# Way to the first experts: normed rows on VectorE, and two modulation groups moved there

## The chip, the cores and the metric

The kernel runs on one core of a Trainium2 chip. The metric is the time of one execution on the device in microseconds, the median over repeated executions. A core has TensorE (PE, matrix products), VectorE (DVE), ScalarE (ACT), GpSimd (POOL) and SyncE (SP, which here only issues transfers), each with an instruction stream of its own, kept in step by semaphores. Sixteen DMA engines move data between main memory and the on-chip memory. In the profile's rows PEclk is the clock granted to TensorE, as a share of 2.4 GHz; 0.50 is its lower level, 1.2 GHz.

## The reference, cut to what matters

A network of two blocks of layers on 256 tokens and 256 context tokens of width 1024, in float32. Each layer of the first block is modulated by a condition vector, mixes (linear recurrence and differential attention in layer 0, windowed attention in layer 1), and ends in a mixture of 16 experts of which every token takes two:

```python
mod = (jax.nn.silu(c) @ w_ada + b_ada)[:, None, :]
mod_c = (jax.nn.silu(c_ctx) @ w_ada + b_ada)[None, None, :]
sh1, sc1, g1, sh2, sc2, g2 = jnp.split(mod, 6, axis=-1)
...
x = x + g1 * y
h2 = rms_norm(x, norm_ffn_g[layer]) * (1.0 + sc2) + sh2
...
tokens = jnp.concatenate([h2.reshape(-1, d_), hc2.reshape(-1, d_)], axis=0)
f = routed_moe(tokens, router_w, router_b, moe_w_gate[layer], moe_w_up[layer], moe_w_down[layer])
...
# routed_moe
aff = jax.nn.sigmoid(jnp.dot(h2d, router_w).astype(F32))
sel = (aff + router_b.astype(F32)).reshape(n_tok, N_GROUPS, EXPERTS_PER_GROUP)
group_score = jnp.sum(lax.top_k(sel, TOP_K)[0], axis=-1)
grp = jnp.argmax(group_score, axis=-1)
...
hid = jax.nn.silu(xblk @ w_gate[e]) * (xblk @ w_up[e])
return hid @ w_down[e]
```

The weights `ada_w` of a layer are 1024 x 6144, so the modulation of both layers is 50 MB of weights for two condition vectors. The modulation of layer 1 is not needed before layer 1.

## The kernel before

The weights come from main memory in tiles of 128 x 2048 float32 (1 MB) that share a pool `W` of 14 slots; `wload` issues every one of them on SP's queue, in the order of the program, and an issue waits until the slot it takes has been released. Larger buffers take slots of the same pool: `XG` (two), the broadcast rows `rows2` (two), the gate rows `g1`. A scheduler orders the instructions of each engine ahead of time from the order of the program and the dependences; at run time each engine runs its list in order.

A modulation group, `ada_group(layer, i)`, covers two of the six parts of a layer's modulation: 8 tiles of `ada_w`, four matmuls to a tile (`pm`, line 364, in float32, which takes two passes, so 8 records in the trace), sums to `M` on VectorE (367), four transposes (375) and small copies to the tiles `AT`, `BT`, `ST`, `GT`. Its stationary operand is `scT`, the silu of the two condition vectors, made once at the start by `ada_setup` from two small loads to `cT`. `layer0` holds the groups in a list `extra` and hands out pieces by `more(n)`, n pairs of tiles at a time: in the linear recurrence, and in the attention `diff_attn` before each of its four blocks of 128 queries (`more(3)`). In the attention a head is two score matmuls (`sp`, 965), exponentials (ScalarE, 974), a scaled copy (978), the difference of the two softmaxes (VectorE, 979), transposes (982), and the product with the values (`ob`, 986). The first eight heads have 512 keys, the last eight 256.

Behind the output projection X gets the gated result: `tt` (VectorE, 770), and the addition to X (771), for two of the four row tiles of the second half on GpSimd. The router takes X's transposes and squares (`router_half`), `rstd` (573), and the logits `lg` (575 to 579), and ScalarE makes the sigmoid `aff` (582). `x_gain` forms X times a gain row in `XG` on GpSimd (561). In `ffn` ScalarE multiplies `XG` by `rstd` (1169) and GpSimd adds the shift row (1171); the rows go to main memory as `h2d` (1173), from where the later experts gather theirs. In `route` VectorE finds the two experts of every token: `sel` (1002), comparisons `cmp` (1012, 1013), a mask `mk` (1024), and TensorE counts places from it (`pp`, 1032 to 1036). The first expert's rows are gathered by matmuls with a one-hot matrix `hu` (`first_x`, 1262), and then the experts run: gate `G`, up `U` and down `Y`, each weight tile split by ScalarE (`wh`, 188) and VectorE (`wl`, 189) into two parts, three matmuls for each product (209 to 211). `preload` issues the first 7 tiles of expert 0 early, four of gate and three of up.

Of the kernel before, what the change touches and what calls it, by code (L numbers as in the profile page):

```python
# [11 lines left out]
F32 = mybir.dt.float32  # L12
# [5 lines left out]
OP = mybir.AluOpType  # L18
AX = mybir.AxisListType

P = 128
# [65 lines left out]
class Kern:  # L87
# [233 lines left out]
    def ada_setup(self):  # L321
        nc, wk, a = self.nc, self.wk, self.a
# [5 lines left out]
        nc.vector.memset(self.scT, 0.0)  # L328
        nc.scalar.activation(self.scT[:, :, 0:2], cT, AF.Silu)
        self.gmix = self.C.tile([P, 2, 8], F32, name="gmix")  # L330
# [20 lines left out]
    def ada_group(self, layer, i, bank=False):  # L351

        nc, wk, ps = self.nc, self.wk, self.ps
# [3 lines left out]
        for k in range(8):  # L357
            w = self.wload(W, k, 1, i * 2048, 2048)
            if not bank and k % 2 == 0:
                pm = ps.tile([P, 512], F32, name="pm", tag="tp", bufs=self.tpb)  # L360
            elif bank and k == 0:
                pm = ps.tile([P, 512], F32, name="pm", tag="mm", bufs=2)
# [15 lines left out]
        for r in range(2):  # L378
            v = mT[:, :, :, r].rearrange("p c j -> p j c")
            T = lambda nm: self.C.tile([P, 8], F32, name="%s%d%d" % (nm, layer, r))  # L380
            h = lambda t: t.rearrange("p (j c) -> p j c", j=2)
# [203 lines left out]
    def layer0(self):  # L585
        nc, tc, a = self.nc, self.tc, self.a
        with ExitStack() as st:
# [14 lines left out]
            extra = [self.ada_group(l, i, l == 1) for l, i in ((0, 1), (0, 2), (1, 0), (1, 1), (1, 2))]  # L602
# [146 lines left out]
            for c in range(2):  # L749
# [18 lines left out]
                for t in range(4):  # L768
                    tt = wk.tile([P, 512], F32, name="tt", tag="t2", bufs=self.t2b)
                    nc.vector.tensor_tensor(tt, o[t], g1[t // 2][:, cs], op=OP.mult)  # L770
                    (nc.gpsimd if c and t % 2 else nc.vector).tensor_tensor(self.X[t][:, cs], self.X[t][:, cs], tt, op=OP.add)
# [168 lines left out]
    def diff_attn(self, qT, kT, va, Y, more):  # L940
# [16 lines left out]
        for t in range(4):  # L957
            more(3)
# [31 lines left out]
    def route(self, NT, CB):  # L990
# [53 lines left out]
        nc.vector.tensor_copy(mxi,mx)  # L1044

# [99 lines left out]
    def ffn(self, layer, NT, CB, rs, after, side=None):  # L1145
# [3 lines left out]
        with ExitStack() as st:  # L1149
# [12 lines left out]
            if big:  # L1162

                shift = lambda t: self.rows2[0][:, t // 2]
                self.last_st = self.last_lg
                for t in range(NT):
                    h = self.XG[t]
                    with tc.issue_after(self.last_af) if t > 1 else ExitStack():
                        last = nc.scalar.mul(h, h, self.rstd[:, t:t + 1]).ins
                for t in range(NT):  # L1170
                    nc.gpsimd.tensor_tensor(self.XG[t], self.XG[t], shift(t), op=OP.add)
                    with tc.issue_after(last):
                        nc.scalar.dma_start(h2d[t * P:(t + 1) * P, :], self.XG[t])
# [19 lines left out]
            R = self.route(NT, CB)  # L1193
# [1256 lines left out]
```

## Time and profile before

| | |
|---|---|
| time, median of 3 runs | 2206.57 us (2206.48 to 2207.69) |
| the profiled execution's own time | 2207.79 us |
| its span in the trace | 2205.8 us |
| mean granted clock of TensorE | 0.963 |
| busy: PE, DVE, ACT, POOL | 1989.6, 1414.7, 954.8, 342.1 us |
| loads of `ada_w` as 1 MB tiles | 40 |

TensorE is busy 90% of the span, but that is a mean over stages with different limits; the stages around the change have to be read one by one. The attention of layer 0 lies at 308 to 398 us, the output projection up to 450, the way to the first experts (router, routing, gathering of the first rows) from 450 to 488, and the experts of layer 0 follow from 488.

### The profile page before, as it was taken

The numbers are of one execution on the slowest core, as the hardware profiler recorded it, in microseconds if no ns is written. First come the engines' busy times: TensorE is split into PE (matmuls) and PEld (weight loads), VectorE is DVE, ScalarE is ACT, GpSimd is POOL, SyncE is SP. The second block draws the span as 40 slices with busy tenths as digits, with TensorE's granted clock in tenths as the row PEclk, the third lists the DMA queues.
The fourth block names the chain that finished last, engine by engine and source line by source line (L and its number), as shares of the span: only waits on it lengthen the run. The fifth ranks groups of instructions, "written<-read, shape, count | busy, mean of one in ns | idle before, by whom it ended". The sixth has DMA issues, their size and how long they took to land. (4 is left out here: it accounts for less than half of the span.)

```text
span 2205.8 us, 30075 instructions
## 1 busy us (share of the span) xinstructions
PE 1989.6 (90%) x11466; PEld 1361.1 (62%) x11467; DVE 1414.7 (64%) x2524; ACT 954.8 (43%) x1435; POOL 342.1 (16%) x384
## 2 busy tenths in 40 slices
PE   6999979969999999996979979999888889888998
PEld 2877654747778888774776543333333266776997
DVE  3457666569999999898857654232331169676767
ACT  2434325437778788774645520000000032455443
POOL 1201122140000000016030021010100025231111
PEclk9999989979999999998989989999999999989999
DMA  8444467759999999996533479999999953425460
GB/s 260 124 144 135 137 251 269 273 178 357 361 376 384 385 385 388 378 345 236 191 103 71 175 293 386 364 408 409 409 408 409 409 188 124 154 96 172 163 209 20
DMA packets 191307, 580.52 MB, mean 263 GB/s; under 512 B 18736, under 2 KB 49904, under 8 KB 186032
## 3 DMA queue, kind: packets, MB, share of 16 engines
q1 hardware_dynamic: 176656, 550.03, 67.5%
q0 software_dynamic: 7760, 23.26, 3.3%
q10 hardware_dynamic: 6736, 5.21, 0.8%
q8 instruction: 93, 1.52, 0.3%
q14 instruction: 62, 0.51, 0.1%
HBM read 568.41 MB, written 10.03 MB: 262 GB/s over the span
## 5 line engine op out<-in xcount | busy, mean ns | idle before, releaser
L189 DVE TENSOR_TENSOR wl<-wch,wh 128x1024 fp32r<-128x1024 f32 x518 | 649.0, 1274 | 142.9 <-ACT wh L188 126.7
L188 ACT CAST wh<-wch 128x1024 fp32r<-128x1024 f32 x524 | 545.4, 1053 | 300.1 <-PE pj L210 63.6
L211 PE MATMUL pj<-h,wl 128*128 128x256 f32 x448 | 131.6, 295 | 5.8 <-DVE wl L189 5.7
L209 PE MATMUL pj<-h,wh 128*128 128x256 f32 x448 | 131.5, 295 | 2.6 <-ACT h L487 1.2
L210 PE MATMUL pj<-h,wh 128*128 128x256 f32 x448 | 130.9, 293 | 0.0
L1323 ACT ACTIVATE s<-G 128x512 f32<-128x512 f32 x16 | 9.6, 598 | 273.0 <-PE G L1309 273.0
L1309 PE MATMUL G<-wch,xT 128*64 128x512 f32 x512 | 125.5, 617 | 1.5 <-DMA wch<-in_moe_w_gate_dram 1.2
L1309 PE MATMUL U<-wch,xT 128*64 128x512 f32 x512 | 119.9, 600 | 4.5 <-DMA wch<-in_moe_w_up_dram 4.0
L1309 PE MATMUL Y<-wch,hTe 128*64 128x512 f32 x488 | 110.4, 597 | 6.6 <-DMA wch<-in_moe_w_down_dram 5.0
L210 PE MATMUL U<-wl,xu 128*128 128x512 f32 x256 | 103.6, 405 | 8.6 <-DVE wl L189 7.6
L210 PE MATMUL Y<-wl,hu 128*128 128x512 f32 x256 | 103.3, 403 | 7.9 <-DVE wl L189 7.7
L210 PE MATMUL G<-wl,xu 128*128 128x512 f32 x256 | 103.0, 403 | 6.5 <-DVE wl L189 6.3
L209 PE MATMUL U<-wh,xu 128*128 128x512 f32 x256 | 102.4, 400 | 3.4 <-ACT wh L188 3.4
L209 PE MATMUL Y<-wh,hu 128*128 128x512 f32 x256 | 100.8, 394 | 2.6 <-ACT wh L188 2.4
L209 PE MATMUL G<-wh,xu 128*128 128x512 f32 x256 | 101.4, 396 | 0.0
L211 PE MATMUL U<-wh,xu 128*128 128x512 f32 x256 | 101.2, 395 | 0.0
L211 PE MATMUL Y<-wh,hu 128*128 128x512 f32 x256 | 100.6, 393 | 0.0
L211 PE MATMUL G<-wh,xu 128*128 128x512 f32 x256 | 100.2, 391 | 0.0
L211 PEld LDWEIGHTS pj<-h,wl 128*128 128x128 f32 x448 | 89.1, 199 | 9.1 <-DVE wl L189 6.6
L209 PEld LDWEIGHTS pj<-h,wh 128*128 128x128 f32 x448 | 89.1, 200 | 6.0 <-issue 2.1
L210 PEld LDWEIGHTS pj<-h,wh 128*128 128x128 f32 x448 | 89.4, 199 | 1.9 <-issue 1.7
L209 PE MATMUL mm<-wh,hTh 128*128 128x256 f32 (+1 forms) x256 | 81.3, 319 | 3.6 <-DVE Y L693 1.9
(669 smaller groups left out, 4221.6 us busy)
## 6 DMA issues: line engine op xcount, KB each, us to landing
wch<-in_moe_w_gate_dram SPq DMA_DIRECT2D x128, 1024.0 KB, 7.6
wch<-in_moe_w_up_dram SPq DMA_DIRECT2D x128, 1024.0 KB, 8.9
wch<-in_moe_w_down_dram SPq DMA_DIRECT2D x125, 1024.0 KB, 7.5
wch<-in_ada_w_dram SPq DMA_DIRECT2D x40, 1024.0 KB, 6.7
wch<-in_even_w_in_dram SPq DMA_DIRECT2D x34, 1024.0 KB, 5.7
wch<-in_odd_w_in_dram SPq DMA_DIRECT2D x16, 1024.0 KB, 5.4
wch<-in_even_w_out_dram SPq DMA_DIRECT2D x10, 1024.0 KB, 5.2
wch<-in_ada_w_dram SPq DMA_DIRECT2D x32, 256.0 KB, 6.6
```

Source lines behind the costliest of these rows:

```text
L188: self.last_h = nc.scalar.copy(h, v).ins
L189: self.last_l = e.tensor_tensor(l, v, h.bitcast(F32), op=OP.subtract).ins
L209: m(out, lh, rh, start=first, stop=False, skip_group_check=chk)
L210: m(out, lh, rl, start=False, stop=False, skip_group_check=chk)
L211: self.last_m = m(out, ll, rh, start=False, stop=last, skip_group_check=chk).ins
L1309: self.last_m = nc.tensor.matmul(out[f * 64:f * 64 + 64, :], x[:, k, :], v[k - k0][:, f * 512:(f + 1) * 512], start=(k == 0), stop=(k == 7 ...
L1323: self.last_s = nc.scalar.activation(s, G, AF.Silu).ins
```

## The change

Three things are done.

The rows `XG` are now completed by one VectorE operation to a tile, (XG x rstd) + shift (a `scalar_tensor_tensor` of 128 x 1024), in a function `normed` that `route` calls behind its counting; ScalarE's four multiplications and GpSimd's four sums go. All additions to X run on VectorE.

Two of the three modulation groups of layer 1, (1,0) and (1,1), leave the list `extra`. They become `ada_late`, and the program runs them behind `route`, in one bank of the tag `Y`. The attention's blocks ask for one pair of tiles each and not three.

The pool that held `scT` is closed by then, so `scT` is made again: `conditions` loads `cT` a second time by two small transfers on ScalarE's queue and takes the silu. GpSimd and not VectorE sets the memory of `scT`.

```diff
-    def ada_setup(self):
+    def conditions(self):
         nc, wk, a = self.nc, self.wk, self.a
         cT = wk.tile([P, 8, 2], F32, name="cT", bufs=1)
...
-        nc.vector.memset(self.scT, 0.0)
+        nc.gpsimd.memset(self.scT, 0.0)
         nc.scalar.activation(self.scT[:, :, 0:2], cT, AF.Silu)
+
+    def ada_setup(self):
+        nc, wk, a = self.nc, self.wk, self.a
+        self.conditions()
...
-            extra = [self.ada_group(l, i, l == 1) for l, i in ((0, 1), (0, 2), (1, 0), (1, 1), (1, 2))]
+            extra = [self.ada_group(0, 1), self.ada_group(0, 2), self.ada_group(1, 2, "mm")]
+            self.ada_late = [self.ada_group(1, i, "Y") for i in (0, 1)]
...
-                    (nc.gpsimd if c and t % 2 else nc.vector).tensor_tensor(self.X[t][:, cs], self.X[t][:, cs], tt, op=OP.add)
+                    nc.vector.tensor_tensor(self.X[t][:, cs], self.X[t][:, cs], tt, op=OP.add)
...
-            more(3)
+            more(1)
...
         mxi=w.tile([1,1],I32,name="mxi",tag="mxi",bufs=1)
         nc.vector.tensor_copy(mxi,mx)
+        if normed:
+            normed()
...
-                shift = lambda t: self.rows2[0][:, t // 2]
                 self.last_st = self.last_lg
-                for t in range(NT):
-                    h = self.XG[t]
-                    with tc.issue_after(self.last_af) if t > 1 else ExitStack():
-                        last = nc.scalar.mul(h, h, self.rstd[:, t:t + 1]).ins
-                for t in range(NT):
-                    nc.gpsimd.tensor_tensor(self.XG[t], self.XG[t], shift(t), op=OP.add)
-                    with tc.issue_after(last):
-                        nc.scalar.dma_start(h2d[t * P:(t + 1) * P, :], self.XG[t])
+
+                def normed():
+
+                    for t in range(NT):
+                        h = self.XG[t]
+                        nc.vector.scalar_tensor_tensor(h, h, self.rstd[:, t:t + 1], self.rows2[0][:, t // 2], op0=OP.mult, op1=OP.add)
+                        nc.scalar.dma_start(h2d[t * P:(t + 1) * P, :], h)
...
-            R = self.route(NT, CB)
+            R = self.route(NT, CB, normed if big else None)
+            if big:
+
+                self.conditions()
+                for g in self.ada_late:
+                    for _ in g:
+                        pass
```

TensorE's list at the end of the attention, before, among the last heads (`sp`, `tp<-c_ident,pe` and `ob` are the heads' scores, transposes and products; `pm` the modulation tiles, four matmuls each):

```order
L965 MATMUL sp_3381<-hu_489,hu_487 128x256
L364 MATMUL pm<-wch,scT 32x512 x4
L965 MATMUL sp_3382<-hu_489,hu_487 128x256
L965 MATMUL sp_3404<-hu_489,hu_487 128x256
L965 MATMUL sp_3405<-hu_489,hu_487 128x256
L364 MATMUL pm<-wch,scT 32x512 x20
L375 MATMUL tp<-c_ident,M 128x128 x4
L982 MATMUL tp<-c_ident,pe 128x128 x4
L986 MATMUL ob<-hu_491,aT 128x128 x4
```

And the same place in the changed kernel, up to the transposes of `Y` for the output projection:

```order
L972 MATMUL sp_3245<-hu_489,hu_487 128x256
L993 MATMUL ob<-hu_491,aT 128x128 x2
L972 MATMUL sp_3246<-hu_489,hu_487 128x256
L972 MATMUL sp_3268<-hu_489,hu_487 128x256
L989 MATMUL tp<-c_ident,pe 128x128 x2
L972 MATMUL sp_3269<-hu_489,hu_487 128x256
L989 MATMUL tp<-c_ident,pe 128x128 x2
L993 MATMUL ob<-hu_491,aT 128x128 x4
L989 MATMUL tp<-c_ident,pe 128x128 x2
L993 MATMUL ob<-hu_491,aT 128x128 x2
L989 MATMUL tp<-c_ident,pe 128x128 x2
L308 MATMUL tp<-c_ident,Y 128x128 x4
```

The five tiles and the transposes of `M` behind the last scores are gone there. In the whole attention 26 tiles become 10: four instead of five ahead of the first scores, and six instead of 21 behind them.

ScalarE's list from the last copy for the router to the first rows of the first expert, before:

```order
L548 COPY xrT<-tp 128x4x128
L1169 ACTIVATE xg<-xg,rstd 128x1024
L582 ACTIVATE aff<-lg 128x64
L1169 ACTIVATE xg<-xg,rstd 128x1024 x3
L1173 DMA h2d_3954<-xg 128x1024 x4
L1192 ACT_TABLE_LOAD
L315 CAST xu_3956<-x_4036 128x512 x2
```

and now:

```order
L554 COPY xrT<-tp 128x4x128
L325 DMA cT<-in_c_dram 128x8x1
L326 DMA cT<-in_c_ctx_dram 128x8x1
L1179 DMA h2d_3818<-xg 128x1024
L329 ACT_TABLE_LOAD
L329 ACTIVATE scT<-cT 128x8x2
L1179 DMA h2d_3818<-xg 128x1024
L588 ACT_TABLE_LOAD
L588 ACTIVATE aff<-lg 128x64
L1198 ACT_TABLE_LOAD
L1179 DMA h2d_3818<-xg 128x1024 x2
L315 CAST xu_3820<-x_3896 128x512 x2
```

The sigmoid `aff` now has behind the copies two small loads, the silu, two issues of `h2d` and two table loads ahead of it.

VectorE's list from `rstd` to the selection (`lg` are the logits, `mrow` the shift rows), before:

```order
L573 COPY rstd<-rq_z 128x4
L575 TENSOR_REDUCE lg<-lt 128x64
L576 TENSOR_TENSOR lg<-lg,rq_z 128x64
L579 TENSOR_TENSOR lg<-lg,SB 128x32 x2
L1002 TENSOR_TENSOR sel<-aff,rb 128x4x16
L1004 TENSOR_TENSOR pr<-sel 128x16x2
```

and in the changed kernel:

```order
L579 COPY rstd<-rq_z 128x4
L1178 SCALAR_TENSOR_TENSOR xg<-xg,rstd,mrow 128x1024
L581 TENSOR_REDUCE lg<-lt 128x64
L1178 SCALAR_TENSOR_TENSOR xg<-xg,rstd,mrow 128x1024
L582 TENSOR_TENSOR lg<-lg,rq_z 128x64
L1178 SCALAR_TENSOR_TENSOR xg<-xg,rstd,mrow 128x1024
L585 TENSOR_TENSOR lg<-lg,SB 128x32 x2
L1178 SCALAR_TENSOR_TENSOR xg<-xg,rstd,mrow 128x1024
L1009 TENSOR_TENSOR sel<-aff,rb 128x4x16
```

Four operations on 128 x 1024 elements stand between `rstd` and `sel`, three of them ahead of the last operation on the logits.

In TensorE's list the first three of the moved tiles stand behind the router's transposes, ahead of `pp`, the fourth between `pp` and the gathering matmuls, numbers five to seven among and behind these, and the other nine with the two sets of transposes of `M` between the first expert's matmuls. On SP's queue the 16 loads now stand behind the 7 preloaded tiles of expert 0 and ahead of the rest of its up tiles; before, they stood ahead of the output projection's weights.

## Rows read from the trace of the kernel before

**Rows 1.** Stretches: start:end, length, busy PE, PEld, DVE, ACT, POOL, PEclk, DMA share, GB/s.
```profile
330.00:385.60 55.60, 53.33 (x291) 24.03 (x290) 33.43 (x106) 30.62 (x79) 13.61 (x18) 0.95 0.75 271
385.60:398.00 12.40, 10.03 (x69) 5.52 (x68) 9.64 (x32) 6.45 (x17) 2.89 (x4) 0.86 1.02 345
...
450.40:488.00 37.60, 16.19 (x132) 13.21 (x132) 28.32 (x85) 11.99 (x20) 20.36 (x15) 0.68 0.55 196
488.00:560.00 72.00, 69.46 (x334) 55.16 (x334) 65.92 (x93) 53.67 (x59) 4.06 (x4) 1.00 0.95 350
560.00:900.00 340.00, 336.60 (x1543) 271.56 (x1542) 313.98 (x326) 270.61 (x296) 18.24 (x20) 1.00 1.00 380
1400.00:1700.00 300.00, 266.63 (x1635) 96.66 (x1632) 88.78 (x222) 15.96 (x33) 25.75 (x63) 0.99 1.02 407
```

**Rows 2.** TensorE's timeline in the attention: start, us, line, out<-in, records [idle before].
```profile
331.99 1.93 PE L364 MATMUL pm<-wch,scT 128*32 128x512 f32 x8
...
385.67 4.50 PE L364 MATMUL pm<-wch,scT 128*32 128x512 f32 x40
391.80 0.63 PE L375 MATMUL tp<-c_ident,M 128*128 128x128 f32 x4 [1.63 <-issue]
```

**Rows 3.** TensorE's instructions by line, 300 to 400 us: the modulation tiles.
```profile
L364 PE MATMUL pm<-wch,scT 128*32 128x512 f32 x208 | 32.7, 618 | 0.0
```

**Rows 4.** VectorE's timeline in the attention: the operation that closes a head's softmax.
```profile
328.07 0.75 DVE L979 SCALAR_TENSOR_TENSOR pe<-pe,su 128x512 f32<-128x512 f32 x1
...
364.88 0.75 DVE L979 SCALAR_TENSOR_TENSOR pe<-pe,su 128x512 f32<-128x512 f32 x1 [0.59 <-ACT pe L978]
...
387.99 0.48 DVE L979 SCALAR_TENSOR_TENSOR pe<-pe,su 128x256 f32<-128x256 f32 x1
...
396.59 0.48 DVE L979 SCALAR_TENSOR_TENSOR pe<-pe,su 128x256 f32<-128x256 f32 x1
```

**Rows 5.** Timeline of all engines on the way to the experts.
```profile
456.70 0.66 PE L544 MATMUL tp<-c_ident,xin 128*128 128x128 f32 x4 [2.42 <-POOL xin L771]
...
461.72 0.17 DVE L573 COPY rstd<-rq_z 128x4 f32<-128x4 f32 x1
...
463.15 2.60 DVE L579 TENSOR_TENSOR lg<-lg,SB 128x32 f32<-128x32 f32 x2
...
467.17 6.99 POOL L1171 TENSOR_TENSOR xg<-xg,mrow 128x1024 f32<-128x1024 f32 x3 [0.97 <-ACT xg L1169]
467.27 2.42 DVE L1013 TENSOR_TENSOR cmp<-sel 128x60 f32<-128x60 f32 x1
...
474.14 0.18 DVE L1012 TENSOR_TENSOR cmp<-sel 128x20 f32<-128x20 f32 x1
...
474.61 1.28 ACT L1192 ACT_TABLE_LOAD   x1 [5.46 <-DMA h2d<-xg]
...
475.58 0.23 DVE L1024 TENSOR_TENSOR mk<-oh 128x64 bf16<-128x64 f32 x1
...
477.66 5.88 PE L1262 MATMUL x<-hu,xg 128*128 128x128 f32 x32 [1.26 <-DVE hu L1256]
```

**Rows 6.** VectorE's instructions by line and shape: busy us, mean ns of one.
```profile
L2161 DVE SCALAR_TENSOR_TENSOR xin<-xin,rf,gains 128x1024 f32<-128x1024 f32 x2 | 2.6, 1279 | 0.0
```

**Rows 7.** Tile cT at the program's start; a small load at 60 to 130 us.
```profile
L325 ACTq DMA_DIRECT2D cT<-in_c_dram x1: 460/460/460, 1.4 to 1.4; - x1
...
DMA to landing us min/median/max: 11.8/11.9/12.1
...
fpg<-in_final_norm_g_dram POOLq DMA_DIRECT2D x1, 4.0 KB, 6.4
```

**Rows 8.** Waits of SP's queue, 520 to 900; loads at 450 to 488 us.
```profile
SPq L172 <- DVE wl L189: 315.9, 123, 5.2
...
wch<-in_moe_w_gate_dram SPq DMA_DIRECT2D x4, 1024.0 KB, 6.0
```

More of the change, by code (lines that the diff above doesn't have):

```diff
@@ L360, in ada_group @@
                 pm = ps.tile([P, 512], F32, name="pm", tag="tp", bufs=self.tpb)
+            elif bank == "mm" and k == 0:
+                pm = ps.tile([P, 512], F32, name="pm", tag="mm", bufs=2)
             elif bank and k == 0:
-                pm = ps.tile([P, 512], F32, name="pm", tag="mm", bufs=2)
+                pm = ps.tile([P, 2, 512], F32, name="pm", tag=bank, bufs=1)[:, 0]
             for j in range(4):
@@ L988, in diff_attn, with route @@
             self.head_norm(Y[t][:, 512:], sub, nc.gpsimd if t < 2 else nc.vector)
-    def route(self, NT, CB):
+    def route(self, NT, CB, normed):
         nc,tc,w,ps=self.nc,self.tc,self.wk,self.ps
```

## The prediction

> **What bounds the kernel now.** I read the table of stretches first, because the change touches three stages with different limits [rows 1]; in it the reader is to see the busy times beside the length of each stretch. In the attention of the first layer (330 to 385.6) TensorE is busy 53.3 of 55.6 us while VectorE has 33.4 and ScalarE 30.6: TensorE is the bound, and what is taken from it there shortens the stage. The end of the attention (385.6 to 398) has TensorE busy 10.0 of 12.4 us. On the way to the first experts (450.4 to 488) TensorE is busy 16.2 of 37.6 us at a mean granted clock of 0.68, and the DMA engines 0.55 of the time: here a chain of small operations is the bound. In the experts (488 to 560 and 560 to 900) TensorE is busy 96% and 99%, and the DMA engines 0.95 and 1.00.
>
> Second I read the timelines of single engines. TensorE's shows the price of a modulation tile: 40 records, which are five tiles of four matmuls in two passes, run in 4.50 us, so 0.9 us a tile at the full clock, and one tile took 1.93 us at half the clock [rows 2]. The group of this line has 208 records, 8 to a tile: 26 tiles lie in this stage [rows 3]. VectorE's shows the rhythm of the heads by the operation that closes each softmax: eight heads with 512 keys between 328.07 and 364.88, a step of 5.3 us, then seven with 256 keys up to 387.99 (3.3 us a head on average), and the last one 8.6 us later, at 396.59 [rows 4]. The timeline of the gap [rows 5] shows the chain: TensorE waits 2.42 us for an addition to X on GpSimd and goes on at 456.70, rstd is there at 461.89, the logits at 465.75, the mask mk at 475.81, and the first matmul that gathers rows starts at 477.66.
>
> **The change, term by term.**
>
> (a) *Attention.* Of 26 tiles 10 stay, so 16 tiles and two sets of four transposes (0.63 us each) leave. By the order one tile leaves ahead of the first scores, ten leave between the heads, and the five at the end leave with their transposes. The end: 4.50 us of tiles and 1.63 us of wait ahead of the transposes [rows 2] go, and the last head should close some 2.5 us behind its neighbour and not 8.6: -6. Between the heads: 10 x 0.9 + 0.63 = 9.6 us less for TensorE in a stage that it bounds. I take -6.5 of it, because the heads with 256 keys have a chain of scores, exponentials and transposes of their own, so that two or three of the tiles may have been free. Together -12.5. Bounds: nothing but the end is won (-6), or all of it, 16 x 0.9 + 1.3 + 1.6 = -17.
>
> (b) *The gap.* First the addition to X goes to VectorE, right behind its product; I take 2.2 of the 2.42 us that TensorE waited. Then rstd is there at about 459.7. Four new VectorE operations of 1.28 us (an operation of this form and shape elsewhere in the kernel [rows 6]) follow, three of them ahead of the last logits, with four short ones between, which I put at 0.2 to 0.4 each like mk: 459.7 + 3 x 1.28 + 1.1 = 464.6 us, and the fourth ends at 465.9. The two last additions to the logits, now 2.60 us beside a GpSimd sum, are in the 1.1: a comparison of the same kind takes 0.18 us when GpSimd is idle and some 2.4 us beside its sums [rows 5]. With those sums gone, three comparisons lose 2.2 us each: from the logits to mk it was 475.81 - 465.75 = 10.1 us, of which 3.5 remain, 3.2 of them behind the sigmoid.
> ScalarE has a new chain: two small loads of the condition vectors, issued behind the last copy for the router (at some 455.8, with 0.46 us an issue [rows 7]), a table load, the silu, the issue of a store, a second table load, the sigmoid: 2 x 1.28 [rows 5] and three short steps of 0.3, so 3.4 us behind the landing. The landing is the unknown: 11.8 to 12.1 us at the program's start, 6.4 us for a load of the same size in a quieter stretch [rows 7]. With 6.4 the sigmoid ends at 455.8 + 0.9 + 6.4 + 3.4 = 466.5, just behind the fourth VectorE operation; mk is then done at 469.7, and the gathering matmuls, which now follow it by 1.9 us, could start at 471.6. On TensorE one modulation tile stands ahead of them, whose slot is freed by the fourth VectorE operation (465.9); with a landing of 6.0 us for such a tile [rows 8] and 1 us to run it is through at 473. So -4.7; three tiles that run ahead may keep the clock up, which is at 0.68 here, and I round to -5. Bounds: with a landing of 12 us everything behind the sigmoid is 5.6 us later and the gain is 0 (+1 with a colder clock); with the quick landing and the full clock for the first 32 gathering matmuls, where 5.88 us could halve, it is -8.
>
> (c) *Experts.* Four of the 16 tiles lie in the gap, where TensorE waits anyway. The 12 others and the two sets of transposes stand among the gathering matmuls and those of the first expert, where TensorE is the bound: 12 x 0.9 + 1.3 = 12.1. I take +12 (10 if some slip into the waits of the gathering, 14 if some run at half clock).
>
> (d) *The weight queue.* The 16 tiles (16.8 MB) now stand on the queue of SP behind seven preloaded expert tiles and ahead of the eighth and all later ones. At the 407 GB/s of the stretch from 1400 on [rows 1] that is 41 us; 0.45 x 37.6 = 17 us of idle DMA time in the gap take part of it, TensorE's own 12 us more, and the rest, 12 us, must come out of the lead of the loads. In the experts the queue waits for slots that VectorE frees (315.9 us in all, 123 times [rows 8]), so there is a lead. The eighth tile follows about nine that are not yet loaded when the gathering ends, 9 x 2.6 = 23 us and a landing of 6, so some 29 us. TensorE has until then all of gate and three quarters of up, 84 matmuls at 0.22 us (1543 in 336.6 us, [rows 1]), and nine tiles at 0.9, so 26.6 us. That is 2 us short; but the loads of the first of the nine are under way by then. I take +1 (0 to +8).
>
> At nothing I put the memory set that goes to GpSimd (which has little else there), the sums for M and the copies behind them on VectorE among the first splits (under 2 us, in a stretch where it has 6 us to spare [rows 1]; without that cover they would cost those 2), and the small loads of biases, which nobody waits for.
>
> Sum: -12.5 - 5 + 12 + 1 = -4.5. The profiled execution took 2207.79 us, 1.2 us above the median of 2206.57, so the forecast for the median is **2202 us**.
>
> **Rivals.**
> 1. *The weight queue becomes the bound* (slower). If the lead is eaten, not TensorE's 12 us count but the queue's 41 us less the 17 idle ones: 24. Sum -12.5 - 5 + 24 = +6.5, 2213 us. At the 350 GB/s of the first experts' stretch it is 48 - 17 = 31, and 2220 us. It decides from the point where the eighth expert tile lands after TensorE has finished the third tile of up. For it: the DMA share of 1.00 in the experts, which leaves no time to catch up. Against it: the waits for slots.
> The Trainium skill (DMA: Bandwidth & Descriptors, Specifications) gives about 358 GB/s as a core's limit from HBM. By it the 16.8 MB would take 47 us and the sum would come to about +12, 2219 us, the upper case of this rival. The trace disagrees with it (407 GB/s over 300 us), so I give the upper case 3 in 100.
> 2. *The sigmoid waits for the condition vectors* (no change). With the landing of 12 us (b) is 0, and the sum +0.5: 2207 us. For it: other loads run beside, as at the start. Against it: the 6.4 us.
> The Trainium skill (ScalarE: Activation LUTs, What ACT_TABLE_LOAD costs) has 1.28 us for the load itself, as the row, and somewhat more again for a drain. No row here shows the drain; with it the sigmoid would be some 2.8 us later and the time about 2204 us.
> 3. *The heads' own chain is the bound once the tiles go*, or the clock falls with the thinner work, as for the tile at 331.99: (a) is -6 to -8, the sum 0 to +2, 2207 to 2209 us.
> 4. *The attention is TensorE's throughout:* (a) -17, (b) -5, (c) 12, (d) 0: 2196.6 us.
>
> **Chances.** A measurement here tells about 0.2%, 4.4 us, from no change. The forecast 0.45, its own range 2197 to 2207, of which 0.25 lies below 2202.2 (faster) and 0.20 above; rival 4 0.17 (faster); rival 2 0.12 (same); rival 1 0.20 (slower); rival 3 0.06 (half of it slower, together with some of the bad ends). So faster 0.42, same 0.35, slower 0.23. The range 2193 to 2213 leaves out the upper half of rival 1 and the end of rival 4.
>
> **What would show it.** (a) The last head closes at about 384 and not 396.6, with no group of tiles behind it, and the step between the heads with 512 keys is some 4.3 us. (b) Comparisons of 0.2 to 0.3 us; from rstd to mk some 10 us and not 13.9; the sigmoid released by VectorE or a table load, not long held by a DMA. (c) TensorE without gaps while the tiles run in the first expert. (d) No wait on a load of up or gate above 1 us in the first two experts. It would be wrong if the table load waits long for the condition vectors, if the first up tiles come late, or if the heads keep their step.

## The result and the profile after

The changed kernel took 2223.67 us (median of 4 runs, 2217.69 to 2227.71) beside 2207.13 us for the kernel before (4 runs, 2206.48 to 2211.92): ratio 1.0068, 95% interval 1.0041 to 1.0095. It is slower by 0.7%, above the forecast of 2202 us and above the range. The profiled execution took 2217.69 us, its span 2215.7. It is the fastest of the four, while the profiled one of before lies 0.7 us above its median: the two spans differ by 9.9 us and the medians by 16.5. The stretches below account for the 9.9.

I cut both spans at the same events: the first scores, the last row of gating products tt in the timeline (a pair), the mask mk, the first gathering matmul, and the first silu (tile s) of an expert, which ends its gate. Each number is the difference of two starts in a timeline, in us.

| stretch | before | after | difference |
|---|---|---|---|
| start to first scores | 314.58 | 314.24 | -0.3 |
| attention: first scores to last tt | 135.63 | 120.45 | **-15.2** |
| gap: last tt to mk | 25.37 | 19.68 | -5.7 |
| gap: mk to first gathering matmul | 2.08 | 6.53 | **+4.5** |
| to the second expert's silu | 48.18 | 66.93 | **+18.8** |
| to the sixth expert's silu | 147.28 | 151.38 | +4.1 |
| to the twelfth expert's silu (six experts) | 212.38 | 220.23 | **+7.9** |
| to the sixteenth expert's silu | 173.64 | 172.98 | -0.7 |
| rest, code that is the same | 1146.66 | 1143.28 | -3.4 |

In the rest no effect of the change is shown: over the twenty profiles of this study that stretch took 1143.3 to 1157.6 us. For the same reason the experiments below are read by their stretches first and by their totals second.

The stretches of after, with the columns of [rows 1]:

```profile
330.00:367.90 37.90, 37.27 (x183) 19.37 (x181) 29.07 (x85) 27.13 (x65) 10.02 (x10) 0.89 0.52 172
367.90:380.30 12.40, 9.68 (x47) 6.46 (x48) 11.62 (x48) 9.03 (x30) 3.02 (x4) 0.83 0.41 147
434.70:472.30 37.60, 24.85 (x175) 14.81 (x176) 27.80 (x95) 10.71 (x20) 10.40 (x12) 0.73 0.89 312
472.30:560.00 87.70, 84.25 (x425) 57.11 (x415) 65.97 (x96) 51.74 (x57) 6.86 (x9) 0.98 1.02 410
560.00:900.00 340.00, 330.65 (x1497) 261.63 (x1496) 305.66 (x319) 260.96 (x288) 17.23 (x19) 1.00 0.99 371
```

The reader is to see three things. At the end of the attention TensorE has 2.7 us of air and VectorE 0.8: by these shares the bound has passed to VectorE. In the gap the DMA engines are busy 0.89 of the time instead of 0.55, with the moved loads. And in the last row the granted clock is as before and the DMA share nearly so (0.99 for 1.00), yet TensorE has 6 us less busy time in the same 340 us than in [rows 1].

The heads on VectorE, for [rows 4]:

```profile
327.38 0.74 DVE L986 SCALAR_TENSOR_TENSOR pe<-pe,su 128x512 f32<-128x512 f32 x1
...
358.98 0.74 DVE L986 SCALAR_TENSOR_TENSOR pe<-pe,su 128x512 f32<-128x512 f32 x1
...
377.44 0.48 DVE L986 SCALAR_TENSOR_TENSOR pe<-pe,su 128x256 f32<-128x256 f32 x1
378.90 0.48 DVE L986 SCALAR_TENSOR_TENSOR pe<-pe,su 128x256 f32<-128x256 f32 x1
```

The step of the eight large heads is 4.5 us (5.3 before), and the last head closes 1.46 us behind its neighbour. The gap, for [rows 5], as one timeline of all engines:

```profile
437.83 1.09 PE L550 MATMUL tp<-c_ident,xin 128*128 128x128 f32 x4 [2.29 <-DVE xin L778]
...
445.63 0.17 DVE L579 COPY rstd<-rq_z 128x4 f32<-128x4 f32 x1
...
447.69 1.28 ACT L329 ACT_TABLE_LOAD   x1 [6.09 <-DVE lg L581]
...
448.98 0.22 ACT L329 ACTIVATE scT<-cT 128x16 f32<-128x16 f32 x1
449.22 1.28 ACT L588 ACT_TABLE_LOAD   x1
...
450.18 1.27 DVE L1178 SCALAR_TENSOR_TENSOR xg<-xg,rstd,mrow 128x1024 f32<-128x1024 f32 x1
...
450.51 0.26 ACT L588 ACTIVATE aff<-lg 128x64 f32<-128x64 f32 x1
...
452.43 0.27 DVE L1019 TENSOR_TENSOR cmp<-sel 128x60 f32<-128x60 f32 x1
...
454.37 0.22 DVE L1031 TENSOR_TENSOR mk<-oh 128x64 bf16<-128x64 f32 x1
...
459.03 1.93 PE L370 MATMUL pm<-wch,scT 128*32 128x512 f32 x8 [3.89 <-DMA wch<-in_ada_w_dram]
...
460.90 5.68 PE L1274 MATMUL x<-hu,xg 128*128 128x128 f32 x32
```

From rstd to mk it is 8.7 us instead of 13.9. The sigmoid (aff) runs in the shadow of the fourth normed row. But a modulation tile stands ahead of the gathering on TensorE's queue, waits 3.89 us for its weights and then runs at half the clock, 1.93 us, as the stretch of that tile alone shows (granted clock third from the end):

```profile
459.00:460.90 1.90, 1.87 (x9) 0.20 (x9) 1.36 (x8) 0.00 (x0) 0.00 (x0) 0.50 1.00 423
```

The loads behind this, over 434 to 475 us (last column: median us to landing):

```profile
wch<-in_ada_w_dram SPq DMA_DIRECT2D x13, 1024.0 KB, 8.0
...
cT<-in_c_dram ACTq DMA_DIRECT2D x1, 4.0 KB, 2.6
cT<-in_c_ctx_dram ACTq DMA_DIRECT2D x1, 4.0 KB, 5.7
```

**What differs in the later experts.** No line of the diff touches them, but the order of their instructions is another one. In the kernel before, the sixth to the tenth expert have on TensorE: 13 matmuls of gate, 5 hidden transposes, 11 gate, 3 hidden transposes, 24 gate; 13 matmuls of down, 4 transposes of the next rows, 35 down, **4 transposes of the next rows**, 48 up. After has: 7 gate, 8 hidden transposes, 18 gate, 6 row transposes, 12 gate, 2 row transposes, 11 gate; 48 down; 48 up. On ScalarE and VectorE the evacuations stand among the weight casts accordingly. Now after at the border of down (Y) and up (U), lines of VectorE's and TensorE's timelines by their start (a bracket gives the engine's idle time ahead and what ended it):

```profile
763.80 0.39 PE L211 MATMUL Y<-wh,hu 128*128 128x512 f32 x1
...
764.23 0.75 DVE L1381 TENSOR_SCALAR y<-Y,wrow 128x512 f32<-128x512 f32 x1 [0.41 <-PE Y L211]
764.90 1.22 DVE L189 TENSOR_TENSOR wl<-wch,wh 128x1024 fp32r<-128x1024 f32 x1
...
765.39 0.39 PE L209 MATMUL U<-wh,xu 128*128 128x512 f32 x1
...
766.17 0.50 PE L210 MATMUL U<-wl,xu 128*128 128x512 f32 x1 [0.39 <-DVE wl L189]
```

The output row y needs the last matmul of down, so VectorE waits for it, and the low half wl of an up weight is queued behind y. TensorE is there first and waits. In the order of before, four row transposes stand just there on TensorE and give VectorE the time. From the first matmul of up to the first of gate this expert takes 12.00 us (764.03 to 776.03), the same one in the kernel before 11.38 (755.72 to 767.10): the border makes up 0.6 of the 1.3 us that an expert takes longer. The other 0.7 lies in short gaps of down and gate, which the runs below don't price one by one.

### The profile page after: what moved, and what is told of

Its sections match the earlier page's. It is cut to its first block, busy times and chain, and to the rows that moved or that the text cites. A ratio compares the mean times of both kernels' runs of the same rounds, so it can differ in the third digit from the quotient of the medians.

```text
span 2215.7 us, 30079 instructions
## 1 busy us (share of the span) xinstructions
PE 2002.9 (90%) x11466; PEld 1361.6 (61%) x11467; DVE 1414.0 (64%) x2529; ACT 951.8 (43%) x1434; POOL 329.1 (15%) x380
```

## The experiments

Eighteen kernels ran, each beside the kernel before on its chip (its median 2208 to 2210 us); the ratios are the recorded estimates and not quotients of the two medians. Two theories for the later experts: **O**, the order of evacuations and transposes costs the 1.3 us per expert; **Q**, the 16 moved loads use up the lead of the weight queue. "Pace" is the time from the sixth to the twelfth expert's first silu, by six; "first two" is from the first gathering matmul to the second expert's silu.

| run | total us | ratio, interval | tt to gathering | first two | pace |
|---|---|---|---|---|---|
| (before, profile) | 2206.57 | | 27.45 | 48.18 | 35.40 |
| (after) | 2223.67 | 1.0068, 1.0041 to 1.0095 | 26.21 | 66.93 | 36.71 |
| norm_alone | 2203.53 | 0.9964, 0.9945 to 0.9983 | 21.41 | 48.66 | 35.39 |
| ada_alone | 2229.91 | 1.0089, 1.0066 to 1.0112 | 28.59 | 73.10 | 36.70 |
| moved_no_loads | 2197.08 | 0.9938, 0.9916 to 0.9961 | 23.03 | 56.61 | 35.41 |
| loads_alone | 2226.35 | 1.0057, 1.0036 to 1.0078 | 21.41 | 54.31 | 36.66 |
| moved_behind_gather | 2223.64 | 1.0065, 1.0040 to 1.0091 | 21.64 | 65.27 | 37.31 |
| moved_old_order | 2227.42 | 1.0077, 1.0052 to 1.0103 | 26.09 | 67.32 | 37.04 |
| moved_split_order | 2232.72 | 1.0112, 1.0085 to 1.0140 | 25.85 | 67.39 | 37.34 |
| before_casts_together | 2211.71 | 1.0015, 1.0002 to 1.0028 | 27.49 | 47.90 | 35.72 |
| rows_split_order | 2209.77 | 1.0007, 0.9988 to 1.0025 | 21.41 | 49.12 | 35.49 |
| rows_after_order | 2264.77 | 1.0249, 1.0227 to 1.0272 | 21.40 | 47.65 | 44.15 |
| loads_before_order | 2232.50 | 1.0101, 1.0077 to 1.0124 | 21.41 | 54.27 | 37.79 |
| moved_before_order | 2233.55 | 1.0104, 1.0079 to 1.0128 | 25.93 | 67.12 | 37.82 |
| moved_exact_order | 2220.16 | 1.0047, 1.0030 to 1.0065 | 25.75 | 67.44 | 36.60 |
| rows_after_exact | 2214.06 | 1.0015, 1.0001 to 1.0030 | 21.41 | 47.72 | 36.94 |
| rows_exact_order | 2212.33 | 1.0005, 0.9989 to 1.0022 | 21.40 | 49.07 | 36.60 |
| moved_late_exact | 2211.01 | 1.0007, 0.9993 to 1.0022 | 21.64 | 65.27 | 36.61 |
| moved_late_same_waits | 2206.18 | 0.9976, 0.9956 to 0.9995 | 22.05 | 65.07 | 35.36 |
| rows_after_same_waits | 2210.05 | 1.0009, 0.9991 to 1.0026 | 21.41 | 47.68 | 36.69 |

**Each half alone.** norm_alone leaves the two groups where they were:

```diff
-            extra = [self.ada_group(0, 1), self.ada_group(0, 2), self.ada_group(1, 2, "mm")]
-            self.ada_late = [self.ada_group(1, i, "Y") for i in (0, 1)]
+            extra = [self.ada_group(0, 1), self.ada_group(0, 2)] + [self.ada_group(1, i, "mm") for i in range(3)]
+            self.ada_late = []
```

> The changed kernel with the two modulation groups left in the attention (three tile pairs a block, condition vectors loaded once), so only the rows on VectorE and the additions to X on VectorE are new. TensorE's list in the later experts is that of the kernel before. Theory O (order: the loss sits in the new instruction order of the later experts, 36.7 us an expert and not 35.4, and in the modulation tile that the gathering matmuls wait for): mk comes 5 to 6 us earlier, the gathering matmuls with it, experts as before, so 2200 to 2202 us. Theory Q (the 16 loads on the weight queue are the loss): the same here, since no load is moved. A third, N (the VectorE operations only take the place of the sums): 2205 to 2208.

ada_alone keeps the groups moved and takes back the normed rows:

```diff
-                        nc.vector.scalar_tensor_tensor(h, h, self.rstd[:, t:t + 1], self.rows2[0][:, t // 2], op0=OP.mult, op1=OP.add)
+                        last = nc.scalar.mul(h, h, self.rstd[:, t:t + 1]).ins
...
+                    nc.gpsimd.tensor_tensor(self.XG[t], self.XG[t], shift(t), op=OP.add)
```

> The changed kernel with the rows completed as before (ScalarE's multiplications, GpSimd's sums, two additions to X on GpSimd), so only the two modulation groups are moved. Its list in the later experts is that of the changed kernel. O and Q both: attention -16 us, experts +25 or more, 2218 to 2226 us, so the whole loss or more comes from this part.

The rows alone gain: 27.45 to 21.41 in the gap, nothing lost later. The moved groups alone lose, and they carry the whole loss: +24.9 in the first two experts and the slower pace. In total each lies above what I had expected, norm_alone 1.5 us above 2202 and ada_alone 3.9 above 2226.

**What of the moved groups costs.** moved_no_loads takes all 16 tiles from two loads, and leaves 14 loads out, so it computes other modulations:

```diff
-            w = self.wload(W, k, 1, i * 2048, 2048)
+            if bank != "Y" or not k:
+                w = self.wload(W, k, 1, i * 2048, 2048)
```

> The changed kernel, but each of the two moved groups loads only its first weight tile and uses it for all eight steps: 14 of the 16 loads are left out (the modulation of layer 1 is computed from wrong weights). TensorE does the same work. The list of the later experts falls back to that of the kernel before. O: experts at 35.4 us from the sixth on, and no wait for a landing ahead of the gathering matmuls: 2200 to 2206. Q: the same or better, as no load stands ahead: 2196 to 2203. It is to be read against the kernel with the loads and the old order.

loads_alone is norm_alone with the 16 loads and no matmul:

```diff
+                for j in range(16):
+                    self.wload(self.a["ada_w"][1], j % 8, 1, j // 8 * 2048, 2048)
```

> The normed rows alone, and in the place of the moved groups 16 further loads of 1 MB each into the ring of weight slots, which nothing reads (they repeat loads that this kernel makes elsewhere; no matmul is added). The order on ScalarE and VectorE in the later experts then is that of the changed kernel. Both theories: 36.5 to 37 us per expert later. For the first two experts: my reading so far gives the loads some 10 us and TensorE's added matmuls 8.4, so the second gate activation should come 8 to 12 us later after the last gating product than with the normed rows alone. A rival for this stage, that the queue's lead hides the loads and only the matmuls cost: 0 to 3 us. Total 2216 to 2226 by the first.

In the first two experts the matmuls alone cost 56.61 - 48.66 = 8.0 us, the loads alone 54.31 - 48.66 = 5.7, both together 18.3: they cost more together than the sum of 13.6. My expectation for the loads (8 to 12) was missed: I had put that rest of 4.7 down to them. In loads_alone ScalarE's waits (475 to 560 us) show the rival of the queue once, at the fourth tile of the first expert's up, which is the eighth expert tile; TensorE, which had finished the third, waited with it:

```profile
ACT wh L188 <- DMA wch<-in_moe_w_up_dram: 6.9, 1, 6.9
...
509.91 0.80 PE L209 MATMUL U<-wh,xu 128*128 128x512 f32 x1 [4.79 <-ACT wh L188]
```

The changed kernel has no such wait: there the eighth tile landed at 496.48, and TensorE, with the moved tiles to run, came to it at 506.54. Between the first gathering matmul and the second expert's silu its longest wait is 0.95 us, for a `wl`. The trace of the changed kernel gives the 18.3 (steps from start to start, beside norm_alone): 12.65 us for the 12 tiles and 1.30 for their transposes, +4.7 in the matmuls of gate and up, -0.4 in all else. Of the 4.7 some 1.8 lie in nine changes from expert matmuls to a tile and back, about 0.1 us each way, 1.6 in eight matmuls at half the clock (the granted clock of their stretch is the third number from the end), and the rest in short waits for VectorE:

```profile
516.00:519.40 3.40, 3.40 (x9) 2.63 (x8) 3.06 (x4) 1.62 (x2) 0.00 (x0) 0.50 1.03 412
```

Nor is the 8.0 of the matmuls alone their whole time on TensorE: in moved_no_loads the 64 gathering matmuls took 7.33 us at a granted clock of 1.00, in norm_alone 9.85 at a mean of 0.74. So the two differences need not add up to the third.

Without the loads the pace was 35.4, with them 36.7, but the order changed with them: without loads it was that of before, with them that of after. From here on the question was which of the two it is.

**The tile ahead of the gathering.** moved_behind_gather (on moved_split_order, below) puts the moved tiles from the fourth on behind the gathering matmuls:

```diff
+                with self.tc.issue_after(self.x0_last) if bank == "Y" and (k > 2 or i) else ExitStack():
+                    nc.tensor.matmul(pm[32 * j:32 * j + 32, :], self.scT[:, k, :], w[:, 0, j * 512:(j + 1) * 512],
```

> As the moved loads with the split order, and the fourth and later modulation tiles are held behind the matmuls that gather the first expert's rows; only the first three stay ahead. If the gathering matmuls wait for the landing of the fourth tile (3.89 us of wait and 1.93 us of its own in the changed kernel), they start 4 to 5 us earlier, at 1.9 us behind mk; the fourth tile then adds 1 us later, so 3 to 4 us less than the run with the split order alone. If the loads hold the first expert anyway, nothing is won by its end.

From mk to the gathering it is 1.94 us instead of 6.16, and the second silu comes 6 us earlier counted from the last tt (86.91 for 93.24). So the gathering waited for the landing of that tile and for its run.

**The order, held roughly.** Seven runs pinned transposes and evacuations behind single matmuls or casts, as here the row transposes in moved_old_order:

```diff
+                    with self.tc.issue_after(self.y_mark[q]) if self.y_mark and slot else ExitStack():
+                        nc.tensor.transpose(tp[:, c, :], xg[:, (q * 4 + c) * P:(q * 4 + c + 1) * P], ident)
...
+        self.y_mark = [self.marks[i] for i in ((0, 0), (7, 1))] if CB == 128 else None
```

moved_split_order also takes the two hidden halves apart:

```diff
+                s = self.gate(CB, xT, ld(wg[e + 1]), [(2, lambda: self.hidden_half(old, 0, None)), (4, lambda: self.hidden_half(old, 1, (3, 0)))])
```

before_casts_together puts those halves together in the kernel before; rows_split_order holds the split order in norm_alone; the last three hold the evacuations behind chosen casts (moved_before_order: `self.y_mark, self.y_cast = self.marks[0, 0], self.casts[3]`).

> The changed kernel with all 16 loads, but the transposes of each next expert's rows are held behind the first down matmuls of the current expert, as they stand in the kernel before; ScalarE's and VectorE's lists follow. O: 35.4 to 35.6 us an expert from the sixth on instead of 36.7, so 7 to 9 us less than the changed kernel in the same job. Q: the loads still hold the pace, no more than 2 us less than the changed kernel.

> All 16 loads moved as in the changed kernel. The transposes of each next expert's rows are held behind the first down matmuls, and the two halves of the hidden rows' transposes are held apart (the second behind the tenth gate product), from the fifth expert on. TensorE's, VectorE's and ScalarE's lists there are then those of the kernel before up to one weight cast. In the earlier run with the old place of the row transposes alone the pace stayed at 37.0 us, and there two casts of hidden rows stood back to back on ScalarE. Theory O (order): 35.4 to 35.6 us an expert from the sixth on, about 8 us less than the changed kernel. Theory Q (the loads hold the pace): 36.7 to 37.1 us as before.

> The kernel before with no load moved; from the fifth expert on the two halves of the hidden rows' transposes are asked for together, so that their two casts stand back to back on ScalarE and their two differences on VectorE, as in the changed kernel. Theory O: 36.5 to 37.1 us an expert from the sixth to the twelfth in place of 35.4, 8 to 11 us slower than the kernel before. Theory Q: 35.4, no difference.

> The rows on VectorE alone (no modulation group moved), and the halves of the hidden rows' transposes held apart in all experts. In the kernel before, the experts from the thirteenth on have the list with the casts back to back and take 36.7 to 38.4 us. Theory O: these fall to 35.4 us, 3 to 6 us less than the run with the rows alone, so 2196 to 2201 us. Theory Q: as the rows alone, 2200 to 2204.

> The way to the experts as in the run with the normed rows alone, no weight groups moved. For the experts from the fifth to the twelfth ScalarE's and VectorE's instructions are held to the very order they have in the changed kernel, TensorE's transposes to within a few matmuls of it. Theory O (the order of casts and transposes costs the 1.3 us per expert): 36.5 to 37.3 us per expert between the sixth and the twelfth gate activation, and a total of 2209 to 2217, above the run with the normed rows alone by 6 to 12. Theory Q (the 16 moved loads use up the lead of the weight queue, and the order is only a by-product): 35.4 us per expert and the total of the normed rows alone, 2200 to 2206.

> The 16 unread loads as in the run before it, but from the fifth expert on ScalarE's order is held to that of the kernel before, VectorE's to it but for one hidden-half operation one cast later, TensorE's transposes a few matmuls earlier. Theory O: 35.4 to 35.8 us per expert, 6 to 9 us less at the end than with the loads alone. Theory Q: 36.5 to 37.3 us per expert and no gain over the loads alone.

> The changed kernel, its two groups and their loads where the change has them, but from the fifth expert on ScalarE's order held to that of the kernel before (VectorE's to it but for one hidden-half operation one cast later). Theory O: 35.4 to 35.8 us per expert, the end 6 to 9 us earlier than the changed kernel, a total of 2209 to 2216. Theory Q: 36.5 to 37.3 us per expert and the changed kernel's time or more, 2218 to 2228.

With the moved loads none of them came near 35.4, which by itself spoke for Q. But the four don't decide: counted against the weight casts, the evacuations of rows and hidden halves and the output row stood one cast earlier in all of them than in before. The two without moved loads kept the border of down and up as before; before_casts_together then says only that the place of the hidden halves costs 0.3 us at most, and rows_split_order, whose order on ScalarE and VectorE is that of before, kept 35.5. Its experts behind the twelfth did not fall to 35.4 as I had expected for O (36.8 and 37.4), and its total lies above both expectations. rows_after_order has a fault of its own: the row transposes of the last two experts are left out, and TensorE waited 28 us for wl between 700 and 900 us; I compare it with nothing.

**The order, held exactly.** For the fifth to the thirteenth expert (rows_after_exact: to the eleventh) the instructions of three engines are written out as a chain, each behind the one before it on its engine:

```diff
+        def on(eng, f):
+            with tc.issue_after(chain[eng]) if eng in chain else ExitStack():
+                chain[eng] = f().ins
```

> The changed kernel, but from the fifth to the thirteenth expert every instruction of TensorE, ScalarE and VectorE is held to the very order that the kernel before has in its sixth to tenth expert, cast by cast and matmul by matmul (the runs before this one with a held order had the evacuations one weight cast too early). Theory O: 35.3 to 35.6 us per expert between the sixth and the twelfth gate activation, the end 8 to 14 us earlier than the changed kernel, a total of 2205 to 2213. Theory Q (the moved loads use up the queue's lead): 36.5 to 38 us per expert and 2217 to 2232.

> The normed rows alone, no group moved and no load added, but from the fifth to the eleventh expert all three engines are held to the changed kernel's exact order. Theory O: 36.5 to 37 us per expert, a total of 2211 to 2216. Theory Q: 35.3 to 35.6 us per expert and the total of the normed rows alone, 2201 to 2206.

> The normed rows alone, held to the order that the kernel before has in its sixth to tenth expert, here up to the thirteenth. It is the control of the two runs beside it: both theories give 35.3 to 35.6 us per expert between the sixth and the twelfth gate activation. Theory O also gives the twelfth to the fourteenth this pace, where the normed rows alone take 37.3 and 36.6: 2 to 5 us less at the end, a total of 2198 to 2203; theory Q gives no gain there.

> As the changed kernel held to the exact order, and the moved tiles' matmuls from the fourth on are put behind the matmuls that gather the first expert's rows, as in the earlier run with the moved tiles behind the gathering. Theory O: 35.3 to 35.6 us per expert, and 0 to 4 us less than the run that only holds the order, 2203 to 2211. Theory Q: 36.5 to 38 us per expert, 2215 to 2230.

All four took 36.6 to 36.9, the control rows_exact_order too, which has neither the loads nor another order. Its waits from 669 to 888 us (us in total, times, longest) show why:

```profile
PE U L1480 <- DVE wl L1470: 7.9, 6, 1.3
...
DVE y L1448 <- ACT y L1446: 7.3, 6, 1.2
```

I had issued ScalarE's half of y ahead of VectorE's, so VectorE waited for ScalarE (before: the other way round), 1.2 us per expert, and TensorE 1.3 for the wl queued behind. The runs settle nothing between O and Q, but the control prices one late y: 1.2 us an expert, with no load and no order changed.

**Order and waits as they were.** Only that is turned round; moved_late_same_waits is moved_late_exact, rows_after_same_waits is rows_after_exact with it:

```diff
-                {("Y", 4): [lambda e: lo("x", 0)], ("U", 1): [lambda e: y(e, 0), lambda e: e > self.e0 and lo("x", 1)], ("G", 1): [prod],
+        return ({("U", 1): [lambda e: y(e, 0)]}, {("Y", 4): [lambda e: hi("x", 0)],
...
+                for g in PRE_EV.get((pp, pk), ()):
+                    g(pe)
```

> As the run with the moved groups, their tiles behind the gathering and the held order of before, but VectorE's half of the expert's output row is issued ahead of ScalarE's, so that ScalarE waits for VectorE there and not VectorE for ScalarE (the four runs before had it reversed, their control too, and took 36.6 to 36.9 us per expert). Now the instructions and what each of them waits for are those of the kernel before. Theory O (order and waits of the evacuations set the pace): 35.3 to 35.6 us per expert between the sixth and the twelfth gate activation, a total of 2197 to 2206. Theory Q (the moved loads themselves): 36.4 to 37.5 us per expert, a total of 2208 to 2216.

> The normed rows alone, no group moved, no load added; from the fifth to the eleventh expert the order and the waits of all three engines are those of the changed kernel (the reversed wait of the earlier run is mended here as well). Theory O: 36.4 to 37 us per expert, the end 6 to 9 us later than with the normed rows alone, a total of 2209 to 2214. Theory Q: 35.3 to 35.6 us per expert and 2200 to 2206.

By their pace both meet O and miss Q. All moved loads with the order of before: 212.14 us for six experts, 35.36 each. No moved load with the order of after: 220.13 us, 36.69 each, as after itself (220.23). From the sixth to the twelfth silu the order is thus the cause and the loads are not. For the border, up in the same expert takes 11.99 us in rows_after_same_waits (754.15 to 766.14) and 11.37 in moved_late_same_waits (757.12 to 768.49), as in after and before. The border of down and up in moved_late_same_waits:

```profile
756.76 0.60 PE L1416 MATMUL tp<-c_ident,xg 128*128 128x128 f32 x4
...
757.83 0.74 DVE L1450 TENSOR_SCALAR y<-Y,wrow 128x512 f32<-128x512 f32 x1
758.52 0.69 DVE L1428 TENSOR_TENSOR xu<-tp,xu 128x512 fp32r<-128x512 f32 x1
759.13 3.50 DVE L1472 TENSOR_TENSOR wl<-wch,wh 128x1024 fp32r<-128x1024 f32 x3
...
760.40 0.50 PE L1484 MATMUL U<-wl,xu 128*128 128x512 f32 x1
```

The transposes stand at the border, y starts without a wait, and the U<-wl at 760.40 starts 0.2 us late, with no wait noted.

Of the kernels that leave nothing out, norm_alone (0.9964) and moved_late_same_waits (0.9976) are the fastest; both beat before and after. Their intervals overlap, so which of the two is better is open. Part of the second one's gain is no work of the change: its held order also gives the two experts behind the twelfth silu 35.4 us each, which take 37.3 and 36.7 in before.

## Why the prediction was wrong

**(a) Attention, -12.5 forecast, -15.2 measured.** The mechanism held: no group at the end, a step of 4.5 us where I expected 4.3. The size was too small: between the first and the fifteenth closing it is 50.06 us (327.38 to 377.44) instead of 59.92, so the tiles between the heads gave back all of their 9.6 us on TensorE, as rival 4 had it, and at the end the last head closes 1.46 us behind its neighbour where I took 2.5. The output projection behind them, which the forecast left alone, took 2.2 us more (from the last closing to tt 53.62 before, 55.79 after; why is open). Rival 3 is refuted.

**(b) Gap, -5 forecast, -1.2 measured.** Its first half held in each step: comparisons of 0.27 us and less, 8.7 us from rstd to mk, -5.7 us in all. Rival 2 is refuted: the condition vectors landed in 2.6 and 5.7 us. The Trainium skill (ScalarE: Activation LUTs, What ACT_TABLE_LOAD costs) has a drain beside the table load; the rows show load, silu, load and sigmoid end to end with 0.24 us between an activation's start and the next load, so no drain shows here. The step that failed is the tile ahead of the gathering: "with a landing of 6.0 us for such a tile [rows 8] and 1 us to run it". The fourth normed row, which frees its slot, ends at 451.45, 1.1 us later behind tt than forecast; TensorE starts the tile at 459.03, 7.6 us behind that (8.0 is the median landing there, with thirteen such loads and the rows' stores beside it), after a wait of 3.89; and the tile ran at half the clock, 1.93 us. Landing and clock cost 2.5 us more than forecast, the row 1.1. moved_behind_gather shows the tile's whole price: without it the gathering starts 1.94 us behind mk and not 6.16 (moved_split_order, the same kernel with the tile ahead).

**(c) and (d) First experts, +13 forecast, +18.8 measured.** Two steps failed. TensorE's term, 12.1 forecast, took 13.9 in the trace, 12.65 for the tiles and 1.30 for the transposes. And the matmuls of gate and up, which the sum took at their old pace, took 4.7 us longer, by the changes to the tiles, the half clock and short waits; one of these, 0.52 us at 507.54 for a `wl` that stands on VectorE behind the sum for M, belongs to what was put at nothing. The queue cost TensorE nothing there that the trace shows, since the eighth tile was in place 10 us before its use. Rival 1 had the right sign, but its mechanism, the queue as the bound, did not come about: it shows in loads_alone alone, where TensorE has no tiles to run (4.79 us), and in the later experts the pace is 35.36 us with all loads in place. The queue moved 410 GB/s over 472 to 560 us. The Trainium skill (DMA: Bandwidth & Descriptors, Measured) has a second figure beside the one I cited, 425 GB/s for a core whose neighbour is idle, and the trace is near to that one.

**The missing term.** The step that failed most: the sum had nothing for the third and all later experts, where the profile shows 11.3 us, 7.9 of them between the sixth and the twelfth silu. I took them as untouched because no line of the diff is in them. The order of their instructions changed all the same, because loads were added ahead of them (moved_no_loads has the order of before, loads_alone that of after), and between the sixth and the twelfth silu the order costs the 1.3 us an expert: shown in both directions by the last two runs. The other 3.4 are not shown to be its work. From the second to the sixth silu (+4.1) the order differs as well and ScalarE's noted waits for a load are 0.3 us, but no run holds the order of before there with the loads in place; moved_late_same_waits, held from the fifth expert on, took 151.95 us for that stretch, 4.7 more than before. The Trainium skill (PSUM — Partial Sum Buffer, Engine vs sequencer instructions) calls the queues of ScalarE, VectorE and GpSimd strictly first in, first out; the rows agree, since wl, whose weight half was cast by 763.93, starts at 764.90 as y ends.

**The account.** From forecast to profile: -4.5, then -2.7 for (a), +3.8 for (b), +5.8 for (c) and (d), +11.3 for the missing term, -3.7 for the start and the rest: +10.0, and the spans differ by 9.9. The 6.6 us by which the medians differ more are not accounted for.

## What to carry to other kernels

Where a scheduler writes the order, a change of loads in one stage can reorder stages that the diff doesn't touch: compare the instruction lists of all stages, not of the changed one, before a stage is taken as constant. An operation that needs the last result of one matmul series (here y) should have other TensorE work at that border, or the weight casts queued behind it make TensorE wait in each round (here 0.6 us an expert of the 1.3). And work moved into a gap brings its loads along: the gap hid the matmuls of the tiles that stood in it, but not the landing of the one that stood ahead of the next step.

## What the runs showed that I had not expected

A single wait turned round, VectorE's half of a row behind ScalarE's instead of ahead of it, cost 36.60 - 35.39 = 1.2 us per expert with every instruction in its old place on its engine. And with the moved loads an order close to that of before, its evacuations one cast early and its transposes a few matmuls early, took 37.8 us an expert (moved_before_order), where after's own took 36.7 and the exact one 35.4; which of its waits costs that is open.
